# Block sums over three feature tiles instead of two, and the first head's loads in another order

## The chip, the cores and the metric

One core of one Trainium2 chip runs the whole program. The metric is the device time of one execution in microseconds (us). TensorE is PE here (PEld is its weight load), VectorE is DVE, ScalarE is ACT, GpSimd is POOL, and SP is the engine that issues every DMA of this kernel.

## The reference, cut to what matters

Two layers work on 1024 latent tokens (64 in a row) of width 1024 and 256 context tokens. Layer 0 is a bidirectional mLSTM with 4 heads of 512, layer 1 a pooling mixer. For this change only layer 0 counts:

```
h          = modulate(rmsnorm(x), shift, scale)
xm, z, og  = split(h @ w_in, 3)                # three products of 1024 x 2048
xc         = silu(short_conv(xm))              # 3 taps along the tokens
q, k       = headwise(xc, ...)                 # 4 x 4 blocks
v          = headwise(xm, w_v)
gates      = [q k v] @ w_gate
h_f, h_b   = mLSTM forward and backward        # per head, decays from sums of the gates
y          = (sigmoid(og) * norm(h_f + h_b) + skip * xc) * silu(z)
```

## The kernel before, in words

Every float32 operand is split into a high and a low part (tiles of type fp32r), and a product is three matmuls: high by high, high by low, low by high (`mm3`, L147).

**Feature tiles.** `features(n)` runs for n = 0 to 15; each tile makes 128 columns of xm for all 1280 tokens in three chunks of 512, 512 and 256 tokens (L366). A chunk is 8 steps of `mm3` into a PSUM tile `pa` (three buffers). When a chunk is done, ACT copies it to `xp` (L373) and then its high part to `xmh` (L375), and DVE makes the low part `xml` (L376). After the third chunk come the convolution (L378 to L381) and the split of xc (L388, L389), which runs while PE is already in the next tile. Between the matmuls of tile n+1, PE does the value products of tile n: `token_part` (L395) is a generator, and `features` draws on it at every second step (`next(side)`, L371). Each value product is three matmuls of 144 columns into `pb` (L413); ahead of the tile's end come the gate products with xc (L426 to L430). PE's order here is written out by hand (`manual_schedule`). The other engines and SP each run one queue in order; a planner with a simulated timeline made that order when the program was built.

**Block sums.** z and og are later made by a Strassen scheme, which needs four sums or differences of blocks of the input h. `block_sums` (L509) makes them beside the feature tiles, for k = 0 to 3: it loads two tiles `t0`, `t1` from `h_d` (L517), does four operations on DVE (L520 to L523), and for each of four results makes a split copy: a new tile, an ACT copy (L527), a DVE subtraction (L528), a store to `t_d` (L529). It is a generator too. The main loop draws on it after the features of a tile have been written out:

```python
            if n >= 2:
                for _ in range(3 if n < 10 else 2):
                    next(sums, None)
```

There are six yields for each k, so one k takes two feature tiles: load, four operations and one copy in the first, three copies in the second. The four k lie in n = 2 to 9.

**Buffers.** Tag `S4` has 32 buffers of 4 KB a partition. It holds the split input h (20 of them until the Strassen products end or the features end), `xmh`, `xml`, and the two tiles of the split xc of each feature tile, `t0`, `t1`, the four copies, and later nearly everything in the heads: x (`fetch_x`), q (`make_q`), the decay rows (`load_gates`), v (`fetch_v`). Tag `hn` has 3 buffers of 2 KB.

**Heads.** After the last Strassen product comes the loop over 4 heads of 8 blocks of 128 tokens (L856). Here the planner orders PE as well. For a head the kernel loads xc's high and low parts in three token chunks (ci = 0, 1, 2, `fetch_x`, L684 and L690), two rows of decays broadcast to all partitions (`load_gates`, L711, `S4`) and their context part (`load_ctx_gates`, L704, `hn`), and the values (`fetch_v`, L698); `make_A` and `next_q` make the first q (L733, L734). `decay` (L758) turns the rows into exponentials on ACT (L766 to L771), `score_chunk` (L737) multiplies q by a chunk of xc and DVE applies the decays (L753), `weights`, `turn` and `values` follow.

Of the kernel before, what the change touches and what calls it, by code (L numbers as in the profile page):

```python
# [17 lines left out]
P = 128  # L18
# [3 lines left out]
TC = 256  # L22
# [29 lines left out]
def hybrid_block(ctx: ExitStack, tc: tile.TileContext, xT, ctxT, vecs, w_ada0, w_ada, w_blk, w_krow, blk_mask, w_gate, w_in, b_gate, w_out,  # L52
# [10 lines left out]
    def nm(s):  # L63
        uid[0] += 1
        return f"{s}_{uid[0]}"
# [11 lines left out]
    def tl(tag, shape, dt=F32):  # L77
        n = int(np.prod(shape[1:])) * 4
        assert n <= BYTES[tag], (tag, shape)
        pool = ph["pool"] if tag in PHASED else sb  # L80
        return pool.tile(list(shape), dt, tag=tag, bufs=BUFS[tag], name=nm(tag))
# [3 lines left out]
    def pt_(tag, shape=(P, 512)):  # L85
        return ps.tile(list(shape), F32, tag=tag, bufs=PBUFS[tag], name=nm(tag))
# [4 lines left out]
    def f(t):  # L91
        return t.bitcast(F32)

    def const1(shape, name, dt=F32):
        return ph["pool"].tile(list(shape), dt, name=name)
# [157 lines left out]
    h = {}  # L253
# [94 lines left out]
    def bilinear():  # L348
        wkr = tl("S4", [P, KE, 4, 4])
        nc.sync.dma_start(wkr, w_krow)  # L350
        G.tensor_tensor(wkr, wkr, wb[:, 0, :, None, :].to_broadcast([P, KE, 4, 4]), op=ALU.mult)
        V.tensor_reduce(amat, wkr, axis=AX.X, op=ALU.add)
        V.tensor_scalar(amat, amat, QSCALE, None, op0=ALU.mult)
# [155 lines left out]
    def block_sums():  # L509


        dsh = const1([P, 4, 1], "dsh")
        V.tensor_tensor(dsh, mod0[:, 4:8, 0, 0:1], mod0[:, 0:4, 0, 0:1], op=ALU.subtract)
        for k in range(4):
            t0, t1 = tl("S4", [P, T]), tl("S4", [P, T])
            for t, kk in ((t0, k), (t1, k + 4)):
                nc.sync.dma_start(t, h_d[kk])  # L517
            yield
            b11, b12, b21, b22 = t0[:, :512], t0[:, 512:], t1[:, :512], t1[:, 512:]
            V.scalar_tensor_tensor(b22, b22, dsh[:, k], b12, op0=ALU.add, op1=ALU.subtract)  # L520
            V.tensor_tensor(b12, b12, b11, op=ALU.subtract)
            V.scalar_tensor_tensor(b11, b22, mod0[:, k, 0, 0:1], b11, op0=ALU.add, op1=ALU.add)
            V.scalar_tensor_tensor(b21, b21, mod0[:, k + 4, 0, 0:1], b11, op0=ALU.add, op1=ALU.subtract)  # L523
            yield
            for j, x in ((2, b11), (3, b22), (1, b12), (4, b21)):
                t = tl("S4", [P, 2, 512], F32R)
                S.activation(t[:, 0], x, AF.Copy)  # L527
                V.tensor_tensor(t[:, 1], x, f(t[:, 0]), op=ALU.subtract)  # L528
                nc.sync.dma_start(t_d[j - 1, k], f(t))  # L529
                yield  # L530

    side, parts, sums = iter(()), [], block_sums()
    with ctx0:
        gate_weights()
        for n in range(KE):
            out = features(n, side)
            for _ in side:
                pass
            if n == 1:
                gacc.extend(pt_("pc") for _ in range(3))  # L540
            if n == 2:
                bilinear()
            if n >= 2:
                for _ in range(3 if n < 10 else 2):
                    next(sums, None)
            parts.append(token_part(n, *out))
            if n:
                side = chain(*parts)
                parts = []
# [129 lines left out]
    def fetch_x(hd, h, ci):  # L679
        for part, src in (("xh", xh_d), ("xl", xl_d)):  # L680
            ts = hd.setdefault(part, {})
            if ci == 2:
                t = tl("S4", [P, 4, TC], F32R)
                nc.sync.dma_start(f(t), src[4 * h:4 * h + 4, :, T:TA].rearrange("c p t -> p c t"))  # L684
                for c in range(4):
                    ts[c, ci] = t[:, c]
                continue
            for c2 in range(2):
                t = tl("S4", [P, 2, 512], F32R)
                nc.sync.dma_start(f(t), src[4 * h + 2 * c2:4 * h + 2 * c2 + 2, :, 512 * ci:512 * ci + 512].rearrange("c p t -> p c t"))  # L690
                for j in range(2):
                    ts[2 * c2 + j, ci] = t[:, j]

    def fetch_v(hd, h, j0, j1):
        for j in range(j0, j1):
            for part, src in (("vh", vh_d), ("vl", vl_d)):
                t = tl("S4", [P, 2, DH], F32R)
                nc.sync.dma_start(f(t), src[h, :, 2 * j:2 * j + 2])  # L698
                hd.setdefault(part, []).append(t)

    def load_ctx_gates(h):
        rc = tl("hn", [P, 2, TC])
        for d in range(2):
            nc.sync.dma_start(rc[:, d], a_d[32 * d + h:32 * d + h + 1, T:TA].to_broadcast([P, TC]))  # L704
        return rc

    def load_gates(h):
        out = []
        for d in range(2):
            r = tl("S4", [P, T])  # L710
            nc.sync.dma_start(r, a_d[32 * d + h:32 * d + h + 1, 0:T].to_broadcast([P, T]))  # L711
            out.append(r)
        return out

    def make_A(h):
        ah, al = tl("wh", [P, 4, 32, 4], F32R), tl("wl", [P, 4, 32, 4], F32R)
        r = tl("wr", [P, 4, 32, 4])
        for c in range(4):
            V.tensor_tensor(r[:, c], mask, amat[:, 4 * h + c:4 * h + c + 1].to_broadcast([P, 32, 4]), op=ALU.mult)
        V.tensor_copy(ah, r)  # L720
        V.tensor_tensor(al, r, f(ah), op=ALU.subtract)
        return ah.rearrange("p c a b -> p c (a b)"), al.rearrange("p c a b -> p c (a b)")
# [113 lines left out]
    def start_head(h):  # L836
        hd = {}
        fetch_x(hd, h, 0)
        return dict(h=h, hd=hd)

    def next_q(cur, tp):
        return make_q(cur["hd"], cur["A"], tp)

    def finish_x(cur):
        for ci in (1, 2):
            fetch_x(cur["hd"], cur["h"], ci)

    cur = start_head(0)
    fetch_x(cur["hd"], 0, 1)
    cur["A"] = make_A(0)  # L850
    cur["q"] = next_q(cur, 0)
    cur["R"], cur["rc"] = load_gates(0), load_ctx_gates(0)
    fetch_x(cur["hd"], 0, 2)
    fetch_v(cur["hd"], 0, 0, 5)
    st_prev = st_now = nxt = None
    for i in range(len(seq) + 1):  # L856
        st = None
        if i < len(seq):
            h, ti = seq[i]
            more = h + 1 < NH  # L860
            st = dict(cur, ti=ti)
            decay(st)
            if ti == 7 and more:
                nxt["rc"], nxt["R"] = load_ctx_gates(h + 1), load_gates(h + 1)
            score_chunk(st, 0)
# [33 lines left out]
        if st and ti == 7:  # L899
            cur = nxt  # L900
# [385 lines left out]
```

## Time and profile before

| | |
|---|---|
| median of 3 runs | 2066.52 us (2065.51 to 2070.31) |
| the profiled execution | 2067.85 us |
| its span | 2066.1 us, mean granted clock 0.986 |
| PE busy | 1996.4 us (97%) |
| DVE busy | 1227.0 us (59%) |
| ACT busy | 780.0 us (38%) |
| POOL busy | 291.1 us (14%) |
| DMA | 339.48 MB, mean 164 GB/s |

The span goes from the first to the last instruction; the execution's time has 1.75 us more around it. Busy time says how long an engine held an instruction. Matmuls are pipelined, so a busy PE can still run at half its clock; the granted clock (1.00 is 2.4 GHz, 0.50 is 1.2 GHz) stands in the window views. The span's stages: the start to about 92 us, feature tiles n = 2 to 15 to about 366 us, the z and og products to about 705 us, the heads to about 1232 us, and then layer 1.

### The profile page before, as it was taken

Reading aid. Unit: us, or ns where it says so; the run is one execution under the profiler, and the core shown is the slowest. Engines: PE = TensorE matmul, PEld = TensorE weight load, DVE = VectorE, ACT = ScalarE, POOL = GpSimd, SP = SyncE. Lnnn points to the kernel's source line nnn. Section 1 sums busy time; section 2 is a strip of 40 time slices with the busy share of each in tenths; the row PEclk is TensorE's granted clock in tenths of the full one; section 3 lists DMA queues with packets and bytes.
Section 4 is the critical chain, followed back from the end, with each engine's and each line's share of the span. In section 5 each row is a group of like instructions: output and inputs, shape, how many; then the busy total and the mean of one; then the engine's idle time right before and its main releaser. Section 6 shows DMA issues by size and latency. Waiting matters only on the chain.

```text
span 2066.1 us, 26833 instructions
## 1 busy us (share of the span) xinstructions
PE 1996.4 (97%) x10210; PEld 1684.7 (82%) x10210; DVE 1227.0 (59%) x2028; ACT 780.0 (38%) x1241; POOL 291.1 (14%) x376
## 2 busy tenths in 40 slices
PE   6988899999999999999999999999999999999997
PEld 4877778888888788888888888887888888888897
DVE  4755555687677667667576662444747283744444
ACT  5555555533333432333323322443423132223433
POOL 1000000033322010000000001343000000001275
PEclk9999999999999999999999999999999999999999
DMA  9376666774443754638355334534331312133563
GB/s 367 137 242 232 223 228 214 257 251 126 150 138 123 278 195 138 224 125 276 105 161 212 107 97 138 192 115 166 101 109 52 102 51 92 47 125 131 183 236 127
DMA packets 201986, 339.48 MB, mean 164 GB/s; under 512 B 12508, under 2 KB 116444, under 8 KB 201856
## 3 DMA queue, kind: packets, MB, share of 16 engines
q1 hardware_dynamic: 201856, 337.76, 48.3%
q8 instruction: 80, 1.31, 0.3%
q14 instruction: 50, 0.41, 0.1%
HBM read 234.77 MB, written 102.94 MB: 163 GB/s over the span
## 4 chain that ended last, share of the span: by engine, by line
PE 84%; DMA 6%; DVE 5%; POOL 2%; issue 2%; ACT 1%; SPq 0%; DVEq 0%; POOLq 0%; ACTq 0%
PE pa L136 42%; PE pc L136 32%; PE pb L136 7%; PE pb L794 1%; DMA S<-h_d 1%; DMA wr<-in_w_ada_dram 1%; POOL S L1003 1%; POOL hn L983 1%; DMA S<-in_w_ada_dram 1%; PE pc L825 1%; DVE wl L671 1%; DVE S L915 0%; DMA S<-in_ctxT_dram 0%; DVE T L753 0%; DMA T<-in_bw_out_dram 0%
## 5 line engine op out<-in xcount | busy, mean ns | idle before, releaser
L136 PE MATMUL pa<-S,wh 128*128 128x512 f32 (+1 forms) x2448 | 710.9, 375 | 5.0 <-ACT pt L375 5.0
L136 PEld LDWEIGHTS pa<-S,wh 128*128 128x128 f32 x2448 | 438.5, 191 | 75.2 <-ACT pt L375 6.2
L136 PE MATMUL pc<-S,wh 128*128 128x512 f32 (+1 forms) x1664 | 465.4, 365 | 4.1 <-ACT wh L142 3.2
L136 PE MATMUL pa<-S,wl 128*128 128x512 f32 (+1 forms) x1224 | 454.1, 371 | 3.3 <-DVE wl L144 3.3
L136 PEld LDWEIGHTS pc<-S,wh 128*128 128x128 f32 x1664 | 302.2, 190 | 55.5 <-ACT wh L142 3.4
L144 DVE TENSOR_TENSOR wl<-wr,wh 128x1024 fp32r<-128x1024 f32 (+1 forms) x124 | 147.3, 1188 | 266.6 <-ACT wh L142 265.7
L136 PE MATMUL pc<-S,wl 128*128 128x512 f32 (+1 forms) x832 | 302.9, 366 | 1.0 <-DVE wl L144 1.0
L136 PEld LDWEIGHTS pa<-S,wl 128*128 128x128 f32 x1224 | 232.6, 190 | 43.8 <-DVE wl L144 3.7
L142 ACT ACTIVATE wh<-wr 128x1024 fp32r<-128x1024 f32 (+1 forms) x124 | 124.4, 1003 | 355.7 <-PE pa L136 135.1
L136 PE MATMUL pa<-S,S 128*128 128x512 f32 (+1 forms) x1152 | 249.6, 363 | 5.2 <-DMA S<-xh_d 5.2
L136 PE MATMUL pc<-S,pt 128*128 128x512 f32 x960 | 227.8, 392 | 1.2 <-DVE S L734 0.8
L136 PEld LDWEIGHTS pa<-S,S 128*128 128x128 f32 x1152 | 192.1, 190 | 34.8 <-DMA S<-xh_d 5.6
L136 PEld LDWEIGHTS pc<-S,pt 128*128 128x128 f32 x960 | 178.4, 188 | 38.2 <-DVE S L734 1.4
L136 PEld LDWEIGHTS pc<-S,wl 128*128 128x128 f32 x832 | 157.9, 190 | 26.5 <-DVE wl L144 1.8
L796 ACT ACTIVATE pt<-pb 128x512 fp32r<-128x512 f32 (+1 forms) x96 | 47.9, 524 | 211.5 <-PE pb L794 202.4
L983 POOL TENSOR_TENSOR hn<-hn,pt 128x512 f32<-128x512 f32 (+1 forms) x48 | 77.5, 1617 | 308.9 <-ACT pt L982 307.9
L753 DVE SCALAR_TENSOR_TENSOR T<-pa,T 128x256 f32<-128x256 f32 (+3 forms) x184 | 78.1, 453 | 36.2 <-PE pa L136 31.1
L136 PEld LDWEIGHTS pb<-vv,S 128*128 128x128 f32 x384 | 63.4, 195 | 28.6 <-ACT S L375 11.6
L136 PE MATMUL pb<-S,wh 128*128 128x512 f32 x256 | 78.8, 389 | 0.0
L583 ACT ACTIVATE wh<-T 128x512 fp32r<-128x512 f32 x70 | 41.2, 626 | 96.3 <-PE pc L136 77.7
L136 PE MATMUL pb<-vv,S 128*128 128x144 f32 x384 | 61.1, 267 | 16.8 <-ACT S L375 9.9
L144 DVE TENSOR_TENSOR wl<-T,wh 128x1024 fp32r<-128x1024 f32 x32 | 45.5, 1422 | 47.1 <-ACT wh L142 47.1
(322 smaller groups left out, 2299.5 us busy)
## 6 DMA issues: line engine op xcount, KB each, us to landing
wr<-in_bw_in_dram SPq DMA_DIRECT2D x40, 512.0 KB, 3.6
wr<-in_w_in_dram SPq DMA_DIRECT2D x34, 512.0 KB, 4.6
wr<-in_w_ada_dram SPq DMA_DIRECT2D x32, 512.0 KB, 4.0
wr<-in_w_out_dram SPq DMA_DIRECT2D x32, 512.0 KB, 3.5
T<-in_bw_out_dram SPq DMA_DIRECT2D x32, 512.0 KB, 4.4
S<-y_d SPq DMA_DIRECT2D x28, 512.0 KB, 7.0
vh_d<-T SPq DMA_DIRECT2D x16, 640.0 KB, 4.0
vl_d<-T SPq DMA_DIRECT2D x16, 640.0 KB, 4.6
```

Source lines behind the costliest of these rows:

```text
L136: PE.matmul(out, lhsT, rhs, start=start, stop=stop)
L142: S.activation(h, r, AF.Copy)
L144: V.tensor_tensor(l, r, f(h), op=ALU.subtract)
L583: S.activation(hi, a, AF.Copy)
L671: V.scalar_tensor_tensor(a, w, csil[:, k, 0:1], a, op0=ALU.mult, op1=ALU.add)
L753: V.scalar_tensor_tensor(W[:, lo + sh:hi + sh], p[:, lo - o:hi - o], 1.0, W[:, lo + sh:hi + sh], op0=ALU.mult, op1=ALU.mult, accum_out=dp[ ...
L794: PE.transpose(p[:, j], st["M"][:, s * P:(s + 1) * P], ident)
L796: S.activation(th[:, :n], p[:, :n], AF.Copy)
L825: PE.transpose(p[:, c], hn[:, c * P:(c + 1) * P], ident)
L983: G.tensor_tensor(acc, acc, sq, op=ALU.add)
L1003: engs[1].tensor_tensor(t, t, xr[n // per][:, n % per], op=ALU.add)
```

## The change

One k of the block sums takes three calls instead of six: the load and the four operations in the first, two copies (j = 2, 3) in the second, two (j = 1, 4) in the third. Each feature tile from n = 2 makes one call, so the four k lie in n = 2 to 13. For the first head, the decay rows are loaded ahead of the second chunk of xc, the third chunk directly behind the second, and all of them are written out ahead of `make_A` and the first q; the context decays of the first head go into an `S4` buffer instead of an `hn` buffer. The value products are three matmuls of 144 columns in both kernels.

```diff
@@ block_sums
             for t, kk in ((t0, k), (t1, k + 4)):
                 nc.sync.dma_start(t, h_d[kk])
-            yield
             b11, b12, b21, b22 = t0[:, :512], t0[:, 512:], t1[:, :512], t1[:, 512:]
...
                 nc.sync.dma_start(t_d[j - 1, k], f(t))
-                yield
+                if j in (3, 4):
+                    yield
@@ main loop over n
             if n >= 2:
-                for _ in range(3 if n < 10 else 2):
-                    next(sums, None)
+                next(sums, None)
@@ load_ctx_gates
-        rc = tl("hn", [P, 2, TC])
+        rc = tl("hn" if h else "S4", [P, 2, TC])
@@ first head
     cur = start_head(0)
-    fetch_x(cur["hd"], 0, 1)
+    cur["R"], cur["rc"] = load_gates(0), load_ctx_gates(0)
+    finish_x(cur)
     cur["A"] = make_A(0)
     cur["q"] = next_q(cur, 0)
-    cur["R"], cur["rc"] = load_gates(0), load_ctx_gates(0)
-    fetch_x(cur["hd"], 0, 2)
     fetch_v(cur["hd"], 0, 0, 5)
```

## Rows read from the trace of the kernel before

**Rows 1.** The page: busy time by engine.

```profile
PE 1996.4 (97%) x10210; PEld 1684.7 (82%) x10210; DVE 1227.0 (59%) x2028; ACT 780.0 (38%) x1241; POOL 291.1 (14%) x376
```

**Rows 2.** The chain that ended last: start, length, link; first matmuls of feature tiles.

```profile
110.25 3.08 PE pa L136 x15
...
292.44 2.76 PE pa L136 x12
```

**Rows 3.** Windows over feature tiles: length, busy of five engines, granted clock, DMA share, GB/s.

```profile
156.17:174.86 18.69, 18.68 (x111) 15.83 (x108) 8.54 (x12) 9.77 (x16) 0.16 (x3) 1.00 0.76 254
176.13:201.00 24.87, 20.66 (x109) 17.20 (x110) 15.47 (x25) 12.33 (x20) 0.17 (x3) 0.93 0.63 229
292.44:310.85 18.41, 18.41 (x109) 15.83 (x109) 9.93 (x15) 10.61 (x17) 0.17 (x3) 1.00 0.60 201
```

**Rows 4.** PE's waits from 108 to 295 us: sum, times, longest.

```profile
PE pb L136 <- ACT S L375: 9.9, 4, 3.2
PE pb L136 <- DVE S L376: 6.9, 4, 1.7
PE pa L136 <- ACT pt L375: 5.0, 4, 1.3
```

**Rows 5.** ACT in order of time, third k: start, length, instruction, idle before.

```profile
214.22 0.60 ACT L373 ACTIVATE T<-pa 128x512 f32<-128x512 f32 x1 [0.89 <-PE pa L136]
...
220.38 0.37 ACT L375 ACTIVATE pt<-pa 128x256 fp32r<-128x256 f32 x1
...
225.90 0.63 ACT L527 ACTIVATE S<-S 128x512 fp32r<-128x512 f32 x1 [3.80 <-DVE S L522]
226.43 1.07 ACT L375 ACTIVATE S<-pa 128x512 fp32r<-128x512 f32 x2
```

**Rows 6.** DVE in order of time, the same stretch.

```profile
220.98 0.75 DVE L520 SCALAR_TENSOR_TENSOR S<-S,dsh,S 128x512 f32<-128x512 f32 x1 [2.32 <-DMA S<-h_d]
...
234.23 0.42 DVE L389 TENSOR_TENSOR pt<-T,pt 128x256 fp32r<-128x256 f32 x1
```

**Rows 7.** SP's queue, the same stretch: the second load from h_d.

```profile
213.26 0.99 SPq L517 DMA_DIRECT2D S<-h_d  x1
```

**Rows 8.** ACT in order of time in a feature tile without sums.

```profile
298.66 0.60 ACT L373 ACTIVATE T<-pa 128x512 f32<-128x512 f32 x1 [3.46 <-PE pa L136]
...
301.68 0.42 ACT L388 ACTIVATE pt<-T 128x256 fp32r<-128x256 f32 x1
301.98 0.60 ACT L375 ACTIVATE S<-pa 128x512 fp32r<-128x512 f32 x1
```

**Rows 9.** PE in order of time, first head, with the wait.

```profile
718.90 3.57 PE L136 MATMUL pa<-S,S 128*128 128x256 f32 x8 [5.16 <-DMA S<-xh_d]
```

**Rows 10.** Windows at the first head, columns as in Rows 3.

```profile
718.90:722.00 3.10, 3.10 (x8) 2.52 (x9) 1.29 (x2) 3.10 (x7) 0.29 (x1) 0.50 1.04 408
722.00:726.00 4.00, 4.00 (x16) 3.20 (x15) 0.99 (x6) 2.67 (x6) 0.29 (x1) 0.80 1.02 409
...
695.00:700.00 5.00, 5.00 (x24) 4.14 (x23) 1.54 (x4) 0.63 (x1) 0.00 (x0) 1.00 1.07 381
```

**Rows 11.** SP's queue at the first head.

```profile
695.09 2.02 SPq L690 DMA_DIRECT2D S<-xl_d  x2
...
707.16 0.38 SPq L711 DMA_DIRECT2D S<-a_d  x1
...
709.70 0.49 SPq L684 DMA_DIRECT2D S<-xh_d  x1
```

**Rows 12.** ACT at the first head.

```profile
706.08 0.63 ACT L614 ACTIVATE hn<-pt 128x512 f32<-128x512 f32 x1 [1.98 <-DVE pt L592]
706.62 1.07 ACT L733 ACTIVATE S<-pc 128x512 fp32r<-128x512 f32 x2
707.70 1.28 ACT L768 ACT_TABLE_LOAD   x1
...
716.09 1.15 ACT L770 ACTIVATE T<-S,cst 128x1024 f32<-128x1024 f32 x1 [2.28 <-DMA S<-a_d]
```

## The prediction

> **What bounds the kernel now.** I read the page's busy times first: PE is busy for 1996.4 us, far more than any other engine [rows 1], so a change that removes no matmul can only gain where PE stands still or runs at half its clock. The next views were the chain of waits, for places where PE's matmuls are not linked one to the next, then windows over those places, PE's waits there, and ACT, DVE and SP in order of time. The diff touches two such places.
>
> The first is the feature tiles n = 3 to 10. Their matmuls start at 110.25 us and those of n = 11 at 292.44 [rows 2]: 182.2 us for eight tiles. The tile after them takes 18.41 us at full clock [rows 3], which would make 147.3. The excess is 34.9 us. PE's waits in the stretch sum to 9.9 + 6.9 + 5.0 = 21.8 us, four times each, once for each k of the block sums [rows 4]. The other 13.1 us are half clock behind these waits: of each pair of tiles, the first (156.17 to 174.86) runs at 1.00 in 18.69 us, the second, which begins with the waits, has 0.93 and takes 24.87 [rows 3].
>
> The second place is the first head. At 713.74 PE stops for 5.16 us for the third chunk of xc [rows 9]. Behind it the granted clock is 0.50 for 3.1 us and 0.80 for 4 us [rows 10]: 3.1 + 1.6 us at 1.2 GHz, which cost half, 2.35 us. Together 7.5 us.
>
> **What the waits of the feature tiles wait for.** The reader is to see one odd order on ACT. At 214.22 ACT copies a finished PSUM chunk to `xp` (L373); the high copy of the same chunk (L375) should follow, yet both `S4` copies of that tile come only at 226.43, directly behind the first split copy of the sums (L527), which itself waited 3.80 us with ACT idle. The third chunk's high copy, into a `pt` tile and not into `S4`, is done on time at 220.38 [rows 5]. So neither PSUM nor ACT was the obstacle, but the `S4` buffer. Was none free? By the code there are 32, and 20 hold h; at that point two `xmh`/`xml`, two split xc and `t0`, `t1` make 26. Six are free. What fits is that buffers of one tag are given out in the order in which the program names them: the copy j = 2 is named after the features of tile n and ahead of `xmh` of tile n+1, so L375 may not go ahead of L527. A tile without sums bears this out: there L373 ends at 299.26, but L375 comes at 301.98, directly behind the split of the xc tile named before it (L388) [rows 8], 2.7 us late and harmless.
>
> L527 is late because its data are: L522 makes them, behind L520, which held DVE idle for 2.32 us for the load from `h_d` [rows 6]. So a DMA's latency reaches PE through the order of buffers: PE finds only one `pa` buffer free, then waits for `xmh` (L375) and `xml` (L376), as in rows 4.
>
> **Block sums, part by part.** Loads (8), DVE operations (16), copies (16 on ACT, 16 on DVE) and stores (16) keep their number. What moves is where they are named. In the new first tile of a k, only `t0`, `t1` stand ahead of `xmh` of the next tile, and they have their buffers as soon as SP issues the loads, 213.26 in this k [rows 7]. L375 can then go at about 214, before PE asks for the PSUM buffer at 219.5 (the third chunk's copy freed one at 220.75, and PE had waited at most 1.3 us for it [rows 4, 5]). L520 still waits for the load and DVE stays blocked. In the second and third tile two copies stand ahead of `xmh`; their data were ready a tile earlier, so each costs about 0.6 us of ACT [rows 5] and as much of DVE. A tile leaves ACT 7.8 us and DVE 8.5 us idle [rows 3]. Before, three such copies stood in the second tile of each pair, and PE waited for none of them.
>
> What the blocked DVE still delays is the convolution of that tile. Here its split ends at 234.65 [rows 6], with a sums' copy and two late L376 ahead of it that now go elsewhere. PE, no longer stalled, would want the result for the gate products about a microsecond ahead of the tile's end, 219.5 + 18.4, so at 236.9. The margin is 2.2 us at least, in the k in which DVE waited longest. I take no cost; if a load comes 4 us later than this one, PE waits some 2 us.
>
> The part's bounds: 34.9 us if all goes, and, as a loss, what a held `xmh` costs, below. Between them I take 33.5, since every wait of rows 4 comes from the named order and the first tile of a pair shows what a tile with a load in it takes, 18.69, or 0.3 us over a plain one, four times. The tiles n = 11 to 13, plain so far, take over sums: by the same row nothing on PE. What follows only shifts; the loads back from `t_d` come in the z products, behind n = 15, and so behind the last store.
>
> **First head.** In the named order of `S4`, before: chunk 0 (4 buffers), chunk 1 (4), q (2), decay rows (2), chunk 2 (2), v (10). q cannot be made before PE has finished the last Strassen product; its copies run at 706.62 [rows 12], and the first row load is issued at 707.16, chunk 2 at 709.70, although chunk 1's last loads were issued from 695.09 [rows 11]. The rule of the first part holds here too. After: chunk 0, rows, context rows, chunk 1, chunk 2, then q, then v. SP sends the four row loads ahead of chunk 1's four, and chunk 2's two behind them, all before q. Two loads there took SP 2.02 us [rows 11], so behind 697.1 the four that chunk 1 was pushed back by and chunk 2's two take some 6 us more: chunk 2 is issued by about 703, earlier where SP's stores leave room.
>
> That it lands in time hangs on the DMA engines, which are full here: 381 GB/s at 695 to 700, 408 later [rows 10]. Chunk 2 landed 9.2 us after its issue (709.70 to 718.90 [rows 9, 11]); from 703 that gives 712. PE wants it at 713.74. The gain's bounds are 7.5 us (wait and half clock gone) and a loss of some 4 (below); I take 5.5, since chunk 2 gets out some 7 us earlier, but the margin is under 2 us. One buffer of `S4` stays taken by the context rows through head 0; my count there is at most 31 until chunk 0 is released, so I cost it at nothing.
>
> **The sum.** 33.5 + 5.5 = 39.0 us. Against the profiled execution: 2067.85 - 39.0 = 2028.9. That execution lies 1.3 us above the median of the runs, so as a median 2027.5; I say 2028.
>
> **The rivals.**
> *Sums give only half.* The planner may put L520 or L527 elsewhere, or the loads may wait for buffers, so that one of the two waits stays: -17 - 5.5, 2044. For it: the order is the planner's. Against: the cause of the copy's delay is moved a tile away. 0.14.
> *Table switches.* With the decay rows in early, the exponentials could get between the last sigmoids of og (the last at 706.08). A switch costs 1.28 us [rows 12]; three there and back are 7.7 us of ACT, with some 2 us of idle ahead of each sigmoid to take them. q would be late by 3 to 4 us, and the first head would lose 4 instead of gaining 5.5: 2067.85 - 33.5 + 4 - 1.3, 2037. Against: the exponentials need tiles that the Strassen product's weights still hold. 0.08. The Trainium skill ("ScalarE: Activation LUTs", "Table sets: the hidden batching unit") speaks against such a move: it asks that activations of one set be done together. Its "What ACT_TABLE_LOAD costs" gives 2.66 us for a switch with the drain, by which six would be 16 us; the row shows 1.28 and no drain.
> *DMA is the bound at the head.* The bytes are the same, and the engines full; if chunk 2 waits its share behind everything, PE waits at the same time, and the gain is 33.5: 2033. Against: v's 5 MB, which come last in both orders, are no longer needed to pass first. 0.12, inside the likeliest range. The Trainium skill's "DMA: Bandwidth & Descriptors", "Issuing engines are not separate DMA queues", says that all DMAs interleave on the same 16 engines; by that rule order gains only what stands behind in the queue, and by the row (409 GB/s) it is the same.
> *Slower.* `t0` and `t1` now live three tiles instead of two. If twelve buffers beside h did not do, L375 would be held in every tile from n = 3 to 14, at 34.9 / 8 = 4.4 us each: 52 against 34.9, 17.5 us slower, less the head's 5.5: 2078. It decides from the point where a copy into `S4` finds none free; I count 6 for xm and xc, 2 for `t0`, `t1`, 2 for copies, at most 12 with the next xc. Three copies and `t0`, `t1` did not hold it before. 0.05.
> *No change.* The named order is not the cause and the waits come back in as many places: 0.04.
>
> **How the numbers follow.** Likeliest, both parts work, with or without the DMA's share: 0.69, its own range 2022 to 2036. Table switches 0.08, half 0.14, same 0.04, slower 0.05. The range of 2020 to 2046 takes in the first three and leaves out some 0.15. The bound of what a measurement of this kernel can tell from no change is 0.2%, 4 us. Faster 0.91, same 0.04, slower 0.05.
>
> **What would show it.** Right: in feature tiles n = 3 to 14 PE's waits on L375 and L376 gone, each tile 18.4 to 18.8 us at clock 1.00; L375 ahead of L527 on ACT; L520 still waiting for its load. At the first head, row loads and chunk 2 issued before 701 and no wait of 5 us on xc. Wrong: L375 behind L527 in other tiles, gate products waiting for xc's split, a second table load ahead of the first q, or PE waiting for chunk 1.

## The result, and the profile after

| | before | after |
|---|---|---|
| median | 2068.41 us (2065.51 to 2070.43, 4 runs) | 2038.03 us (2033.82 to 2039.96, 4 runs) |
| the profiled execution, its span | 2067.85 us, 2066.1 us | 2036.71 us, 2035.0 us |
| mean granted clock | 0.986 | 0.992 |

The ratio is 0.9851, 95% interval 0.9829 to 0.9874: 30 us faster, where 39 were forecast (28.5 us against the median of 2066.52 that was given ahead of the prediction). The time lies 10 us above the forecast of 2028, inside the range of 2020 to 2046 and 2 us above the range of the likeliest case, 2022 to 2036.

The page after has these busy times by engine (engine, us, share of the span, instructions). PE does the same 10210 matmuls as in [rows 1] in 13.8 us less. ACT has four instructions more, to which we come back. Line numbers are those of each run's own kernel, so the same line can have a number a little higher or lower than before.

```profile
PE 1982.6 (97%) x10210; PEld 1676.0 (82%) x10210; DVE 1223.2 (60%) x2028; ACT 784.1 (39%) x1245; POOL 300.2 (15%) x376
```

**Feature tiles.** The chain of the changed kernel (start, length, link) at the starts of n = 3 and n = 11:

```profile
109.48 3.08 PE pa L136 x15
...
257.24 2.76 PE pa L136 x12
```

Eight tiles now take 257.24 - 109.48 = 147.8 us, against 182.2 in [rows 2]: 34.4 us less. Windows over two of them, columns as in [rows 3], and all of PE's waits from 100 to 420 us:

```profile
128.22:146.66 18.44, 18.44 (x109) 15.82 (x109) 13.50 (x21) 11.62 (x19) 0.16 (x3) 1.00 0.73 257
146.66:165.07 18.41, 18.41 (x110) 15.84 (x109) 11.03 (x17) 11.50 (x19) 0.16 (x3) 1.00 0.73 258
```
```profile
PE pb L477 <- ACT T L478: 0.7, 3, 0.3
PE pb L477 <- DVE T L470: 0.2, 1, 0.2
```

No wait of [rows 4] is left, and the clock stays at 1.00 where the second tile of a pair had 0.93 in [rows 3]. ACT in order of time shows how near the high copy of xm (L375) still comes. In the tile with a k's loads it no longer waits for the sums, but stands 5.3 us behind the end of its L373, behind a copy of a value product. In the tile after it, two copies of the sums (L526 here, L527 before) do stand ahead of it; they cost 1.0 us, because their data are there.

```profile
171.31 0.60 ACT L373 ACTIVATE T<-pa 128x512 f32<-128x512 f32 x1 [3.66 <-PE pa L136]
...
177.20 0.59 ACT L375 ACTIVATE S<-pa 128x512 fp32r<-128x512 f32 x1
...
195.65 1.14 ACT L526 ACTIVATE S<-S 128x512 fp32r<-128x512 f32 x2
196.69 0.57 ACT L375 ACTIVATE S<-pa 128x512 fp32r<-128x512 f32 x1
```

Both of these L375 end well ahead of the end of PE's tile (PE ends the first of the two at 183.52). The one in [rows 5] came at 226.43, 7 us behind 219.5, where PE asked for the buffer.

**First head.** From the start of n = 11 to the end of the span it is 2066.1 - 292.44 = 1773.7 us before and 2035.0 - 257.24 = 1777.8 us after: 4.1 us lost. The matmuls of the head's next q start at 762.26 before and at 730.89 after; by there 3.8 us of it are lost already, so the loss lies in the head's first blocks. PE's waits from 640 to 780 us (sum, times, longest) say where:

```profile
PE pa L136 <- ACT S L732: 7.5, 1, 7.5
PE pc L136 <- DVE wl L720: 1.9, 1, 1.9
PE pc L824 <- DVE hn L813: 1.4, 1, 1.4
```

The wait of 5.16 us for xc's third chunk [rows 9] is gone. In its place PE waits 7.5 us for q's copy on ACT (L732) and, ahead of it, 1.9 us for q's weights from DVE (L720), which stands on DVE behind an operation (L614) that waits for a sigmoid of ACT. The third wait, 1.4 us, is in the output's transposes. The windows of the wait and of what follows, columns as in [rows 3]:

```profile
674.52:681.97 7.45, 0.00 (x1) 0.00 (x1) 1.02 (x2) 7.42 (x15) 0.58 (x2) 0.77 0.87 321
681.97:688.00 6.03, 6.03 (x22) 5.02 (x23) 3.38 (x5) 0.92 (x2) 0.00 (x0) 0.72 0.91 279
```

PE is idle for the whole first window while ACT is busy for 7.42 of 7.45 us; then PE runs at a mean clock of 0.72. ACT in order of time says with what:

```profile
661.92 0.63 ACT L582 ACTIVATE wh<-T 128x512 fp32r<-128x512 f32 x1 [3.79 <-PE pc L136]
662.57 1.28 ACT L767 ACT_TABLE_LOAD   x1
666.65 0.99 ACT L767 ACTIVATE T<-S,cst 128x128 f32<-128x128 f32 x3 [2.80 <-DMA S<-a_d]
...
669.45 1.28 ACT L613 ACT_TABLE_LOAD   x1
670.75 0.63 ACT L613 ACTIVATE hn<-pt 128x512 f32<-128x512 f32 x1
671.39 1.28 ACT L769 ACT_TABLE_LOAD   x1
...
677.28 1.69 ACT L770 ACTIVATE T<-S,cst 128x256 f32<-128x256 f32 x4
678.99 1.28 ACT L613 ACT_TABLE_LOAD   x1
680.28 1.15 ACT L613 ACTIVATE hn<-pt 128x512 f32<-128x512 f32 x2
681.34 1.55 ACT L732 ACTIVATE S<-pc 128x512 fp32r<-128x512 f32 x3
```

Exponentials of the decays (L766 to L770) now stand ahead of and between the last three sigmoids of og (L613), and all of these ahead of q's copy (L732): 17 exponentials, 9.4 us by their durations, and four table loads. A fifth load follows at 692.12. In [rows 12] the first table load came behind q's copy. What let them go ahead is in SP's queue:

```profile
657.30 2.08 SPq L710 DMA_DIRECT2D S<-a_d  x2
...
667.93 0.36 SPq L683 DMA_DIRECT2D S<-xh_d  x1
```

The row loads (L710) are issued at 657.3 and their data are used at 666.65. Chunk 2 of xc goes out at 667.93. On before's time, later by 292.44 - 257.24 = 35.2 us, that is 692.5 and 703.1, where [rows 11] have 707.16 and 709.70.

### The profile page after: what moved, and what is told of

The parts are those of the page before. It is cut to its first block, busy times and chain, and to the rows that moved or that the text cites. A ratio compares the mean times of both kernels' runs of the same rounds, so it can differ in the third digit from the quotient of the medians.

```text
span 2035.0 us, 26816 instructions
## 1 busy us (share of the span) xinstructions
PE 1982.6 (97%) x10210; PEld 1676.0 (82%) x10210; DVE 1223.2 (60%) x2028; ACT 784.1 (39%) x1245; POOL 300.2 (15%) x376
## 4 chain that ended last, share of the span: by engine, by line
PE 88%; DVE 4%; POOL 3%; DMA 3%; issue 2%; ACT 1%; SPq 0%; DVEq 0%; POOLq 0%; ACTq 0%
PE pa L136 44%; PE pc L136 33%; PE pb L136 8%; PE pb L793 1%; POOL hn L981 1%; POOL S L1001 1%; DMA wr<-in_w_ada_dram 1%; PE pc L824 1%; DVE wl L670 1%; DVE S L913 0%; DMA T<-in_bw_out_dram 0%; DVE wh L231 0%; DVE T L752 0%; DMA T<-in_w_ada_dram 0%; DMA hn<-a_d 0%
## 5 line engine op out<-in xcount | busy, mean ns | idle before, releaser
L136 PE MATMUL pa<-S,wh 128*128 128x512 f32 (+1 forms) x2448 | 703.3, 372 | 0.0
L795 ACT ACTIVATE pt<-pb 128x512 fp32r<-128x512 f32 (+1 forms) x96 | 48.0, 524 | 216.0 <-PE pb L793 210.0
L752 DVE SCALAR_TENSOR_TENSOR T<-pa,T 128x256 f32<-128x256 f32 (+3 forms) x184 | 78.2, 455 | 31.9 <-PE pa L136 30.8
L582 ACT ACTIVATE wh<-T 128x512 fp32r<-128x512 f32 x70 | 41.2, 626 | 96.7 <-PE pc L136 76.4
L806 DVE BATCH_NORM_STATS2 st<-pc 128x6 f32<-128x512 f32 x32 | 22.4, 699 | 85.2 <-PE pc L136 85.2
```

The lines of the kernel that those rows point to most:

```text
L136: PE.matmul(out, lhsT, rhs, start=start, stop=stop)
L582: S.activation(hi, a, AF.Copy)
L752: V.scalar_tensor_tensor(W[:, lo + sh:hi + sh], p[:, lo - o:hi - o], 1.0, W[:, lo + sh:hi + sh], op0=ALU.mult, op1=ALU.mult, accum_out=dp[ ...
L795: S.activation(th[:, :n], p[:, :n], AF.Copy)
L806: V.bn_stats(b6, pv)
```

## The experiments

Each ratio is to the kernel before on the same chip. Runs 1 to 4 stand beside one set of runs of before (median 2067.08 us), 5 to 8 beside another (2066.86), 9 and 10 beside a third (2069.36).

**1. The sums part alone.** The first head as before; the block sums as in the change.

> The block sums over three tiles alone, the first head as before. If the sums give all of their 34.9 us and the head's new load order costs what the two traces show (the distance between the kernels shrinks from 35.1 us at the first q to 31.1 at the end), this runs 4 us faster than the changed kernel: 33 to 36 us under the kernel before. If instead the head's part gains its 5.5 and the sums only some 25, it is 5 us slower than the changed kernel.

Measured: 2035.12 us (2034.14 to 2037.16), ratio 0.9851 [0.9838, 0.9865]. PE's waits from 640 to 780 us keep the one for chunk 2, and the feature tiles have none on L375 or L376:

```profile
PE pa L136 <- DMA S<-xh_d: 5.9, 1, 5.9
PE pc L824 <- DVE hn L813: 0.2, 1, 0.2
```

One part of the change gives the whole of its gain. It is 32.0 us under the kernel before, where 33 to 36 were expected, and the 4 us that it should have been below the changed kernel don't show in the ratios (0.9851 for both, 0.9863 in run 8), whose intervals reach 3 to 5 us to either side. So what the head part costs is read from run 2, and from the waits.

**2. The head part alone.**

```diff
-                if j in (3, 4):
-                    yield
+                yield
...
-                next(sums, None)
+                for _ in range(3 if n < 10 else 2):
+                    next(sums, None)
```

These lines are against the changed kernel; the `yield` behind the loads comes back too.

> The first head's loads alone, the sums as before. By the same theory 3 to 5 us slower than the kernel before, with PE waiting some 7 us for the first q's copy (L733 there) and five table loads on ACT; by the theory of the prediction 5 us faster.

Measured: 2070.39 us (2067.39 to 2073.72), ratio 1.0016 [1.0006, 1.0026]: 3.3 us slower. That is just under the 0.2% that were set as the bound of what can be told, but the whole interval lies above 1. The five table loads are there, and the same waits:

```profile
PE pa L136 <- ACT S L733: 7.5, 1, 7.5
PE pc L136 <- DVE wl L721: 1.5, 1, 1.5
```

**3. No second table.** The changed kernel with another function for the gate og of the last two column tiles, so that no table has to be switched back; the output gate of these columns is not a sigmoid in this run.

```diff
-            S.activation(sg, t, AF.Sigmoid)
+            S.activation(sg, t, AF.Tanh if n == KE - 2 else AF.Sigmoid)
```

> The changed kernel with a tanh in place of the sigmoid of og for the last two column tiles (so their og gate is another function), which the exponentials' table also holds, so that ACT's switches there fall away and its order stays. Theory of the table loads: four loads of 1.28 us, 5.1 us, lie ahead of q's copy and are its delay; PE's wait of 7.5 us falls to some 2.4 us and the kernel gains 5 to 6. Theory of the order: the exponentials themselves stand ahead of q's copy and wait for the decay rows until 675.4 us anyway, so only the load at 679.0 counts; the wait falls by 1.3 us and the kernel gains 1 to 2.

Measured: 2034.32 us (2031.09 to 2035.52), ratio 0.9844 [0.9830, 0.9857], one table load. PE's waits:

```profile
PE pa L136 <- ACT S L732: 4.6, 1, 4.6
PE pc L824 <- DVE hn L813: 1.8, 1, 1.8
PE pc L136 <- DVE wl L720: 0.5, 1, 0.5
```

Of 7.5 + 1.9 = 9.4 us of waiting, 4.6 + 0.5 = 5.1 stay. The switches were 4.3 of it (three loads fewer ahead of q are 3 x 1.28 = 3.8); for the rest there are the exponentials themselves, which still stand ahead of q's copy; run 4 tests them. Neither theory had it whole. The changed kernel did not run beside this one; against its ratios in the result and in run 8 (0.9851 and 0.9863) the gain is 1.4 to 3.9 us, under the 5 to 6 of the theory of the table loads.

**4. The exponentials behind q.** The changed kernel; the loads stay early, but the decays of the first four blocks of head 0 are held until q's second copy is issued (`q_copy` is a list of q's copies, kept for this).

```diff
+            with tc.issue_after(q_copy[1]) if h == 0 and ti < 4 else ExitStack():
+                decay(st)
-            decay(st)
```

> The changed kernel with the exponentials of the first four blocks queued behind the first q's copies on ACT; loads as in the changed kernel. Both theories of the ACT queue: PE's wait of 7.5 us and the half clock behind it (1.7 us) go, 7 to 9 us faster than the changed kernel, if the third chunk has landed by then. If the DMA engines are the bound at this place, PE waits there for a chunk of xc instead, and the gain is under 3 us.

Measured: 2031.15 us (2030.16 to 2032.38), ratio 0.9831 [0.9818, 0.9844], 4.0 us under the sums part alone. ACT now has q's copy at 672.63 and its one table load behind it:

```profile
672.63 1.06 ACT L734 ACTIVATE S<-pc 128x512 fp32r<-128x512 f32 x2
673.72 1.28 ACT L769 ACT_TABLE_LOAD   x1
```

PE waits neither for q nor 5 us for xc (0.4 us are left); the longest that is left there is 3.0 us in the transposes (L795, for DVE's L798). So the early loads are a gain, and ACT's order took it back. Against the changed kernel's ratios (0.9851 and 0.9863) this is 4.1 to 6.6 us, where 7 to 9 were expected; run 9 shows what takes the rest.

**5. Old sums, written out later.** The kernel before, with the sums still over two tiles (up to three copies in one), but drawn on inside `features`, behind the first chunk's copies.

```diff
             V.tensor_tensor(dl, xp[:, xo:xo + w], f(dh), op=ALU.subtract)
+            if ci == 0 and n >= 3:
+                for _ in range(3 if n < 11 else 2):
+                    next(sums, None)
...
-            if n >= 2:
-                for _ in range(3 if n < 10 else 2):
-                    next(sums, None)
```

> The kernel before, first head included, with its two-tile block sums, only drawn on inside the next feature tile, behind the copies of its first chunk, and no longer between two tiles: same work, same number of copies in a tile, another place in the written order. If the written order of buffers is the cause (the copy j = 2 ahead of xmh), ACT's L375 no longer stands behind the sums' copy, PE's three waits go, and the time is that of the sums over three tiles, 32 to 35 us under the kernel before. If the amount of sums' work in one tile is the cause, or the buffers that it holds, half of the gain or more is missing.

Measured: 2036.47 us (2032.28 to 2037.61), ratio 0.9852 [0.9835, 0.9868]. No wait on L375 or L376 is left. ACT in order of time (the sums' copy is L530 here):

```profile
194.03 0.60 ACT L375 ACTIVATE S<-pa 128x512 fp32r<-128x512 f32 x1
...
209.28 0.63 ACT L530 ACTIVATE S<-S 128x512 fp32r<-128x512 f32 x1 [3.77 <-DVE S L525]
...
216.46 0.59 ACT L375 ACTIVATE S<-pa 128x512 fp32r<-128x512 f32 x1
216.94 1.67 ACT L530 ACTIVATE S<-S 128x512 fp32r<-128x512 f32 x3
```

The first copy still waits 3.77 us for late data, as L527 did in [rows 5] for 3.80, and three copies still stand in one tile. But the first L375 of the tile in which the first copy is written goes ahead of it (194.03), and the next tile's (216.46) goes ahead of the other three. The first copy's wait is over (209.28) before the next tile's first chunk is copied (L373, 209.82). The place in the written order was the cause. Spreading the sums over three tiles was not needed.

**6. Four copies in one tile.** Two tiles for a k: loads and the four operations in the first, all four copies in the second.

```diff
             for t, kk in ((t0, k), (t1, k + 4)):
                 nc.sync.dma_start(t, h_d[kk])
-            yield
...
                 nc.sync.dma_start(t_d[j - 1, k], f(t))
-                yield
+            yield
...
-                for _ in range(3 if n < 10 else 2):
-                    next(sums, None)
+                next(sums, None)
```

> The kernel before with all four copies of a k in its second tile, load and operations alone in the first; still two tiles for each k. Written-order theory: no copy that waits for the load stands ahead of xmh any more, so as fast as three tiles, 32 to 35 us under the kernel before, with at most some us lost to four ACT copies in a row. Work-in-one-tile theory: four copies in one tile are worse than three, PE waits there, and most of the gain is missing.

Measured: 2033.60 us (2031.36 to 2036.08), ratio 0.9836 [0.9820, 0.9852], no wait in the feature tiles. ACT makes four copies ahead of L375:

```profile
177.17 2.18 ACT L526 ACTIVATE S<-S 128x512 fp32r<-128x512 f32 x4
179.26 0.57 ACT L375 ACTIVATE S<-pa 128x512 fp32r<-128x512 f32 x1
```

They cost 2.1 us there and nothing on PE. What must not stand ahead of L375 is a copy whose data are late; copies as such may.

**7. Chunk 2 first, rows behind q.**

```diff
     cur = start_head(0)
-    cur["R"], cur["rc"] = load_gates(0), load_ctx_gates(0)
     finish_x(cur)
     cur["A"] = make_A(0)
     cur["q"] = next_q(cur, 0)
+    cur["R"], cur["rc"] = load_gates(0), load_ctx_gates(0)
```

> The changed kernel with the first head's chunks 1 and 2 ahead of the first q and the decay rows behind it, as before. No exponential can then get ahead of q's copy and no table switch falls there; PE no longer waits for chunk 2 but for a PSUM buffer, until the rows are in: a wait of some 3 us instead of 5.9 (sums alone) or 7.5 + 1.9 (the change). 4 to 6 us faster than the changed kernel, and no better than with the exponentials queued behind q.

Measured: 2030.36 us (2027.52 to 2033.86), ratio 0.9821 [0.9803, 0.9839]: the lowest ratio of all, 8.7 us under the changed kernel on the same chip. Chunk 2 leaves at 663.50 and the rows at 673.58, behind the start of q's copies at 671.51; the only table load ahead of the exponentials comes at 681.08. SP's queue, and PE's one wait there:

```profile
663.50 0.49 SPq L683 DMA_DIRECT2D S<-xh_d  x1
...
673.58 0.32 SPq L710 DMA_DIRECT2D S<-a_d  x1
```
```profile
685.19 5.05 PE L136 MATMUL pa<-S,S 128*128 128x512 f32 x14 [4.76 <-DVE T L752]
```

Now the rows are late. They land 7.0 and 7.8 us after their issue, the exponentials begin at 682.38, and until they are done DVE (L752) cannot apply the decays and free the PSUM buffer that the next scores want. So chunk 2 was the part that had to move, and moving the rows ahead of q was harmful as long as nothing held the exponentials (runs 4 and 9 move the rows too). But with the rows behind q a wait of 4.8 us stands in for one of 5.2. Expected were a wait of some 3 us and 4 to 6 us under the changed kernel: the wait is longer, and the time still lower than that.

**8. The changed kernel again,** on the chip of 5 to 7.

> The changed kernel itself, on the same chip as the three others, for the comparison with them: 29 to 33 us under the kernel before; 2 to 5 us slower than with the sums alone, by the waits for q's copy (7.5 us) and its operand (1.9 us) against the wait for chunk 2 (5.9 us).

Measured: 2039.09 us (2037.76 to 2041.22), ratio 0.9863 [0.9848, 0.9878], with PE waiting 7.5 us on L732 as before. It is 27.8 us under the kernel before, a little less than the 29 to 33 expected, and 2.6 and 5.5 us above runs 5 and 6, which have the sums mended and the old head.

**9. Both orders mended,** beside **10,** the sums part alone on the same chip. Run 9 loads chunks 1 and 2, then the rows, all ahead of q, and holds the exponentials as in run 4.

```diff
     cur = start_head(0)
-    cur["R"], cur["rc"] = load_gates(0), load_ctx_gates(0)
     finish_x(cur)
+    cur["R"], cur["rc"] = load_gates(0), load_ctx_gates(0)
     cur["A"] = make_A(0)
```

> The changed kernel with chunks 1 and 2 of xc loaded first, the decay rows behind them and still ahead of the first q, and the exponentials of the first four blocks of head 0 held on ACT until q's copies are issued. If the exponentials' place on ACT is all that the head part got wrong, and the PSUM wait of the order with q ahead of the rows (4.8 us on L752) came from rows issued only behind q, then here there is one table load, no wait on q's copy, none on xc, and the wait on L752 is under 2 us: 3 to 5 us below the kernel with the sums part alone, 2029 to 2032, and level with or just below the two earlier mended versions. Rival: the transfers are the limit, and every order of loads leaves about 4 us of waiting somewhere in the first blocks: then the waits again sum to 3 to 5 us at another line, and the time is 2030 to 2033, 2 to 4 below the sums part alone.

> The sums part alone once more, on the same chip as the kernel beside it, so that what the head's order is worth is read from one chip: 2034 to 2037, with PE waiting 5.9 us for the third chunk of xc, as before the change. If the head's loads were worth nothing, the two would be within 2 us of each other.

Measured: 2033.36 us (2030.20 to 2035.05), ratio 0.9827 [0.9813, 0.9842], and 2036.31 us (2034.38 to 2038.17), ratio 0.9843 [0.9830, 0.9857]: the head is worth 3.0 us here, 4.0 in run 4. The distance fits both theories; the time is 0.4 us above the rival's range and 1.4 above the other's. One table load, nothing on L752, 0.3 us on xc; but a wait of 3.0 us comes again, at 716.40. PE and then DVE of run 9:

```profile
716.40 1.11 PE L795 MATMUL pb<-ident,T 128*128 128x128 f32 x4 [3.04 <-DVE pt L798]
```
```profile
707.98 1.28 DVE L670 SCALAR_TENSOR_TENSOR wl<-wr,csil,wl 128x1024 f32<-128x1024 f32 x1 [2.47 <-DMA wr<-in_w_ada_dram]
...
711.40 1.25 DVE L798 TENSOR_TENSOR pt<-pb,pt 128x512 fp32r<-128x512 f32 x2
...
714.05 1.28 DVE L670 SCALAR_TENSOR_TENSOR wl<-wr,csil,wl 128x1024 f32<-128x1024 f32 x1
...
715.93 0.42 DVE L798 TENSOR_TENSOR pt<-pb,pt 128x256 fp32r<-128x256 f32 x1
```

The rival was right that 3 to 5 us of waiting stay at another line (3.4 + 0.3). Its cause, the transfers as the limit, is not shown: from 710.11 to this L798 DVE is never idle, so the wait is for DVE's queue. In it stand decays (L754), q's weights (L718) and the modulation of a layer (L670), which had waited 2.47 us for a weight load at 707.98. Which of these is to blame was not tried.

The same run shows what the mended order is worth by itself. Counted from the start of n = 11 (258.99 and 292.44), PE is 7.0 us ahead of before at the transposes of the first block (695.30 and 735.72), and 3.1 us at the next q (725.70 and 762.26). The difference lies in the wait on L798 and in a clock of 0.58 over the 3.6 us behind it (716.40 to 720.00).

The intervals of runs 4, 7 and 9 overlap, so they can't be ranked; all three lie below the changed kernel of run 8.

## Why the prediction was right, and where it failed

**The sums: right in cause and size.** The term was 33.5 us, with 34.9 as its upper bound; the trace gives 34.4. It had left 1.2 us for the tiles with loads, which took 0.28 us over a plain one at a clock of 1.00 [rows 3] (so the 13.1 us that it read as half clock were not all that). These did not stay either: such a tile takes 18.45 us now (165.07 to 183.52). The cause read from [rows 5] and [rows 8], that L375 may not go ahead of a copy that is named before it and whose data wait for `h_d`, is shown by run 5, which changes the place and keeps the late copy and the three copies in one tile. Run 6 shows that the amount of work ahead of L375 was no cause either, up to 2.1 us of it. Run 1 has the gain without the head. Two details differed. L375 did not move up to its L373; it stayed 5.3 us behind, and PE didn't mind. And "L375 ahead of L527" held in the tile with the loads alone; in the next, both copies stand ahead of it, at a microsecond, as the working of the term (not its list of signs) had it. Whether buffers are granted in written order, or the planner keeps the order of the instructions, no run separates: run 5 moves both.

**The tiles n = 11 to 13, and `t0` and `t1` held for three tiles: right.** These tiles take sums now without a wait; the rival by which `S4` runs out (2078) is excluded by the waits of the feature tiles.

**The head: wrong in sign.** The term was a gain of 5.5 us; the trace shows a loss of 4.1, and run 2 a loss of 3.3 by itself (0.0016 of 2067, by the interval 1.2 to 5.4). The first links held: chunk 2 went out at 703.1 on before's time (forecast 703 in the working, before 701 in the list of signs), and PE waited for no xc. The step that failed is in the rival that the prediction put at 0.08, table switches. It was set aside with "the exponentials need tiles that the Strassen product's weights still hold". The trace says otherwise: the first exponentials ran at 666.65, as soon as their rows had landed, while three sigmoids were still to come; ACT had read the last of those tiles (L582, `wh<-T`) at 661.92. The prediction's list of signs has "a second table load ahead of the first q"; there were four. The rival's price was good, a loss of 4 and 2037 us, against 4.1 and 2038.03; so the time was that of a case which had 0.08, and the range held it since it reached to the other cases. The chance of 0.69 lay on a case that did not come. That the time fell inside the range was luck, as far as the head goes.

The rival's mechanism was half of the story. It counted switches (7.7 us of ACT, 3 to 4 us late). Run 3 takes them away and 5.1 of 9.4 us of waiting stay: 9.4 us of exponentials in ACT's queue delay q's copy too. Run 4 moves the exponentials alone and both go. The prediction also read "no drain" from [rows 12], which can't show it: the activation behind that load waited 3.84 us for its rows. The changed kernel's rows do show it (below). The Trainium skill ("ScalarE: Activation LUTs", "Table sets: the hidden batching unit") asks that activations of one set be kept together; the trace agrees, with five table loads here against one in runs 3, 4, 7 and 9.

The forecast by its terms, 39.0 us, thus splits into 34.4 - 4.1 = 30.3 in place of 33.5 + 5.5; the spans differ by 31.1, of which 0.8 is the earlier start of n = 3 (110.25 and 109.48).

**DMA as the bound at the head: not borne out.** Run 7 has chunk 2 in time with the same bytes. But even where the exponentials wait, the head gives 3.0 and 4.0 us against the sums part alone (runs 9 and 4), and not 7.5: the 7 us do come, and the next wait (L798, in run 7 L752) takes some back. So the prediction's 5.5 asked too much even of its own case. What the context rows' move from `hn` to `S4` does by itself was not tried; it is in run 2 and not in run 1.

## What to carry to other kernels

Where a planner or a program hands out queue places in written order, write first what is needed first, and never a step with late data ahead of a step that frees a buffer of the critical engine; how much work stands there mattered less (2.1 us of copies cost nothing here). Before you load something earlier, ask what its arrival lets go ahead: on an in-order engine the early data drew 9.4 us of work and four table loads in front of the one copy that PE needed. Hold such work behind that copy explicitly, or load the data behind it.

## What the runs showed of the hardware that had not been expected

Table loads are 1.28 us each time, five times in one head, and the next activation starts 0.02 us behind (669.45 + 1.28, then 670.75): no drain shows. The start of n = 3 varies from 109.48 to 113.16 us over twelve profiles in which the code up to there is the same. It goes with the granted clock between 20 and 40 us: 0.91 after (109.48), 0.83 before (110.25), 0.74 in run 8 (113.16). Two profiles of one kernel (runs 1 and 10) differ by 3.1 us behind the start of n = 11 as well (1773.0 and 1776.1). Differences of 2 to 3 us between single profiles are therefore read here only together with the medians. Behind the wait of 7.45 us the clock was 0.72 over 6.03 us: a new wait on PE has a second price behind it, as the old one had in [rows 10].
